# A two-layer transformer block on one core: the weight sums of its seven-product matmuls, and the output sums of its down blocks, made another way

## The chip, the cores and the metric

The kernel runs on one core of a Trainium2 chip. The metric is the device time of one execution in microseconds. Lower is better.

## The reference

Two layers on 512 tokens of width 1024 (batch 1), in float32. Layer 0 mixes tokens by chunked spatial gating, layer 1 by forgetting attention with 12 heads; both add attention on 256 memory rows. Each layer ends in a gated feed-forward of hidden width 2816, which is where the change lies:

```python
f = rmsnorm(h, ln_ffn_pre[layer])
f = (jax.nn.silu(f @ w_ffn_gate[layer]) * (f @ w_ffn_up[layer])) @ w_ffn_down[layer]
h = h + rmsnorm(f, ln_ffn_post[layer])
```

## The kernel before, in words

A float32 product is made of three matmuls in a rounded format: `mm3` multiplies high part by high part, low by high and high by low. `split` makes the parts of a tile: ScalarE rounds it to `hi` (a cast, line 239) and VectorE subtracts, `lo = src - hi` (line 239 too). So each 128x512 block of weights costs one ScalarE and one VectorE instruction before TensorE can use it. The pairs of parts have eight buffers each.

**Sevens.** The feed-forward's gate and up products run as 2x2 block products in seven multiplications instead of eight (the Winograd form of Strassen's scheme). A `Seven` handles two blocks of 128 hidden columns of one weight: it loads two raw tiles of 128x1024 by SyncE's queue (`loaded`, line 144; four raw buffers, so two sevens' worth), which hold the quadrants a11, a12 and a21, a22. `sums` makes four sums of quadrants on VectorE (lines 1040, 1042, 1044, 1045). The products run in the order 1, 7, 6, 2, 5, 4, 3, twelve matmuls each, into three PSUM tiles `x`, `p` and `q`. Between them ScalarE carries a finished partial from one PSUM tile to another (`carry`, line 1055). `end` adds the rest on VectorE (lines 1083 and 1084) and hands the rows on: for a gate, line 1171 and the SiLU of line 1172; for an up, lines 1178 and 1180. `FirstSeven` is the same without the scheme's full chaining, for the first pair of a layer.

**Groups and down blocks.** After the first two hidden blocks, which are done plainly, a layer has five groups of four blocks, made by four sevens: gate, up, gate, up. `Inner` combines each pair of gated rows for the down product (lines 1207 to 1216); for the first pair of a group it makes some low parts "aside", with a transfer on POOL's queue that adds (`split_aside`, `flo`). After each of the first four groups `down_sevens` multiplies by the down weights, again in seven products, each with two units (`DownSeven` a and b, one per pair). Unit a loads its quadrants into two raw tiles, unit b into four plain tiles `wd`. A unit's product `n` on two PSUM outputs is six matmuls 512 wide. The outputs `chain`, `shared`, `lows` and `ups` are two PSUM tiles each. They are added to the eight running sums `ys[tb][dh]` in SBUF in two ways: `put` copies a tile by ScalarE and adds it by transfers on POOL's queue (`y<-yo`, line 1268), and `final` adds it on VectorE (line 1271).

POOL also makes the reciprocal square roots of the norms between the stages (`rsqrt`, line 260), in the same queue as its transfers.

Each engine runs its own instructions strictly in order. The order is made when the program is built: instructions are placed by program order and by when a model of the machine finds their inputs ready, so that an instruction can be placed ahead of an earlier one. `tc.high_priority()` moves instructions forward in this. A wait that lasts longer than modelled holds back whatever is placed behind it on the same engine.

Of the kernel before, what the change touches and what calls it, by code (L numbers as in the profile page):

```python
# [11 lines left out]
ALU = mybir.AluOpType  # L12
# [28 lines left out]
def hybrid(ctx: ExitStack, tc: tile.TileContext, i: dict, out: bass.AP):  # L41
# [20 lines left out]
    def plain(s, shape=(P, T), dt=F32):  # L62
        return yp.tile(list(shape), dt, tag="y", name=name(s))
# [174 lines left out]
    def split(src, hi, lo, eng=None):  # L238
        last_parts[:] = A.copy(hi, src), (eng or V).tensor_sub(lo, src, hi)  # L239
# [22 lines left out]
    class Norm:  # L262
# [31 lines left out]
        def sums(self, tb, cols):  # L294
            return [self.acc[:, c + tb * P : c + (tb + 1) * P] for c in range(0, T, self.width)]
# [722 lines left out]
    class Seven:  # L1018
# [5 lines left out]
        def __init__(self, xs, src, rows):  # L1024
            self.xs, self.rows = xs, rows
            w1, w2 = loaded(src(0)), loaded(src(1))
            self.a = [w[:, d : d + 512] for w in (w1, w2) for d in (0, 512)]
            self.x, self.p, self.q = ps("mm", s="x"), ps("lg", (P, 256), s="a"), ps("tr", (P, 256), s="e")
            self.s1, self.s2 = prob("s1"), prob("s2")

# [5 lines left out]
        def sums(self):  # L1036

            a11, a12, a21, a22 = self.a
            self.s3 = temp("s3")
            V.tensor_add(self.s3, a11, a21)  # L1040
            self.w1 = self.parts(a11)
            V.tensor_add(a21, a21, a22)
            self.w2 = self.parts(a12)
            V.tensor_add(a11, a21, a11)
            V.tensor_add(a12, a11, a12)

        def product(self, o, w, n, more=False):
# [102 lines left out]
    def feed_forward(layer, phase, xp, meanwhile=None):  # L1150
# [36 lines left out]
        def split_aside(src, hi, lo, aside):  # L1187
            if not aside:
                return split(src, hi, lo)
            A.copy(hi, src)  # L1190
            A.activation(lo, hi, AF.Copy, scale=-1.0)
            G.dma_start(lo, src, accum_op=ALU.add)

        class Inner:

            def __init__(self, k, aside):
                self.k, self.aside, self.u = k, aside, {}

            def __call__(self, row, u):
                self.u[row] = u  # L1200
# [19 lines left out]

        class DownSeven:

            def __init__(self, pair, spare):
                self.x = pair.x
                if spare:
                    a11, a12, a21, a22 = (plain("wd").rearrange("p (m c) -> p m c", m=4) for _ in range(4))
                    for n, a in enumerate((a11, a12, a21, a22)):
                        last_load[0] = nc.sync.dma_start(
                            a, i["w_down"][layer, 4 * (n // 2) : 4 * (n // 2) + 4, :, pair.k + n % 2, :].rearrange("m p c -> p m c"))
                else:  # L1230
                    raws = []
                    for dh in range(2):
                        raw = wp.tile([P, 1024], F32, tag="raw", name=name("raw"), bufs=4)
                        last_load[0] = nc.sync.dma_start(
                            raw.rearrange("p (m c) -> p m c", m=4),
                            i["w_down"][layer, 4 * dh : 4 * dh + 4, :, pair.k : pair.k + 2, :].rearrange("m p k c -> p m (k c)"))
                        raws.append(raw.rearrange("p (m k c) -> p m k c", m=4, k=2))
                    a11, a12, a21, a22 = (r[:, :, x, :] for r in raws for x in range(2))
                self.w = {4: a22}
                s3 = temp("s3").rearrange("p (m c) -> p m c", m=4)  # L1240
                V.tensor_sub(s3, a11, a21)
                self.w[1] = self.parts(a11)
                V.tensor_add(a21, a21, a22)
                self.w[2] = self.parts(a12)
                V.tensor_sub(a11, a11, a21)
                V.tensor_add(a12, a11, a12)
                self.w.update({3: a12, 5: a21, 6: a11, 7: s3})

            def parts(self, src):
                pair = pair_of_parts()  # L1250
                split(src, *(t.rearrange("p (m c) -> p m c", m=4) for t in pair))
# [10 lines left out]
        def down_sevens(pairs):  # L1262

            def put(x, *where):
                some = prob("yo")
                A.copy(some, x)  # L1266
                for tb, dh in where:
                    G.dma_start(ys[tb][dh], some, accum_op=ALU.add)  # L1268

            def final(x, tb, dh):  # L1270
                V.tensor_add(ys[tb][dh], x, ys[tb][dh])

            a, b = DownSeven(pairs[0], False), None
            chain = [ps("lg", s="yc") for _ in range(2)]
            a.product(chain, 1, True, False)
            lows = [ps("mm", s="yl") for _ in range(2)]
            a.product(lows, 2, True, False)
            shared = [ps(t, s="ys") for t in ("tr", "tr")]
            a.product(shared, 7, True, False)
            ups = [ps(t, s="yu") for t in ("mm", "lg")]  # L1280
            a.product(ups, 3, True, False)
            b = DownSeven(pairs[1], True)
# [6 lines left out]
            for u in (a, b):  # L1289
                u.product(chain, 6, False, u is b)  # L1290
            for x in range(2):
                A.copy(shared[x], chain[x])
            b.product(ups, 3, False, True)
            for x in range(2):
                final(ups[x], x + 2, 0)
            a.product(chain, 5, False, False)
            a.product(shared, 4, False, False)
            b.product(lows, 2, False, True)
            for x in range(2):
                final(lows[x], x, 0)  # L1300
            b.product(chain, 5, False, True)
            for x in range(2):
                put(chain[x], (x + 2, 0), (x + 2, 1))
            b.product(shared, 4, False, True)
            for x in range(2):
                final(shared[x], x, 1)

        fs = [(act("fhi"), act("flo")) for _ in range(2)]

# [9 lines left out]
        w = [down_weights(layer, 0, dh) for dh in range(2)]  # L1319
# [9 lines left out]
                A.copy(ys[tb][dh], o)  # L1329

        for gi, (k0, k1) in enumerate(groups):
            fs, pairs = [], []
# [25 lines left out]
            down_sevens(pairs)  # L1358


    def layer_b(phase, fp):
# [227 lines left out]
    for tb in range(TB):  # L1589
        end, sums = tail(tb)  # L1590
# [68 lines left out]
```

## Time and profile before

| what | value |
|---|---|
| median of 3 runs | 1103.44 us (1103.33 to 1104.97) |
| the profiled execution's own time | 1101.56 us |
| its span in the trace | 1099.8 us |
| granted TensorE clock, mean | 0.998 |
| TensorE (PE) busy | 1080.4 us, 7266 matmuls |
| VectorE (DVE) busy | 955.7 us |
| ScalarE (ACT) busy | 760.6 us |
| GpSimd (POOL) busy | 107.7 us |
| transfers of the POOL queue (q0, software) | 25.70 MB, 13.3% of the 16 engines' span |
| transfers of the SP queue (q1, hardware) | 116.57 MB, 34.5% |

In rows of the profile a line such as L1040 is a line of the kernel, `out<-in` are its tiles, and the number in brackets at the end of a timeline row is the idle time of the engine before the instruction and what ended it. In rows of windows come the stretch, its length, the busy time of PE, PEld (weight load), DVE, ACT and POOL with counts, the granted clock, the share of the DMA engines and GB/s. In rows of waits come total, times and the longest. Matmuls overlap, so their durations add up to more than the time they take.

### The profile page before, as it was taken

The numbers are of one execution on the slowest core, as the hardware profiler recorded it, in microseconds if no ns is written. First come the engines' busy times: TensorE is split into PE (matmuls) and PEld (weight loads), VectorE is DVE, ScalarE is ACT, GpSimd is POOL, SyncE is SP. The second block draws the span as 40 slices with busy tenths as digits, with TensorE's granted clock in tenths as the row PEclk, the third lists the DMA queues.
The fourth block names the chain that finished last, engine by engine and source line by source line (L and its number), as shares of the span: only waits on it lengthen the run. The fifth ranks groups of instructions, "written<-read, shape, count | busy, mean of one in ns | idle before, by whom it ended". The sixth has DMA issues, their size and how long they took to land.

```text
span 1099.8 us, 19894 instructions
## 1 busy us (share of the span) xinstructions
PE 1080.4 (98%) x7266; PEld 986.5 (90%) x7267; DVE 955.7 (87%) x1906; ACT 760.6 (69%) x1588; POOL 107.7 (10%) x136
## 2 busy tenths in 40 slices
PE   9999999999999989999999999999999999999998
PEld 7998889998989889898988998889998989899896
DVE  7879759999999989896968789868999999989876
ACT  7776578666767657577747788868666766757564
POOL 0000000003030202101000000000003030211200
PEclk9999999999999999999999999999999999999999
DMA  7521331338485655755222654531338575663732
GB/s 270 161 80 52 121 116 39 116 97 211 135 195 150 140 149 133 174 166 162 78 77 65 161 125 122 146 115 39 115 97 200 146 173 139 151 163 93 183 97 77
DMA packets 86298, 143.85 MB, mean 131 GB/s; under 512 B 7028, under 2 KB 50056, under 8 KB 86200
## 3 DMA queue, kind: packets, MB, share of 16 engines
q1 hardware_dynamic: 71480, 116.57, 34.5%
q0 software_dynamic: 14016, 25.70, 13.3%
q8 instruction: 57, 0.93, 0.3%
q10 hardware_dynamic: 704, 0.32, 0.1%
q14 instruction: 41, 0.34, 0.1%
HBM read 105.23 MB, written 2.10 MB: 98 GB/s over the span
## 4 chain that ended last, share of the span: by engine, by line
PE 75%; DVE 9%; DMA 7%; issue 4%; ACT 3%; POOL 1%; SPq 0%; DVEq 0%; ACTq 0%; POOLq 0%
PE y L191 5%; PE y L192 5%; PE y L193 5%; PE ps L191 4%; DMA y<-yo 4%; PE ps L193 4%; PE ps L192 4%; PE a L191 4%; PE a L192 3%; PE a L193 3%; DVE wlo L239 3%; DMA raw<-in_w_gate 3%; PE x L191 2%; PE x L192 2%; PE x L193 2%
## 5 line engine op out<-in xcount | busy, mean ns | idle before, releaser
L239 ACT CAST whi<-raw 128x512 fp32r<-128x512 f32 x444 | 266.2, 619 | 131.3 <-PE x L192 26.2
L239 DVE TENSOR_TENSOR wlo<-raw,whi 128x512 fp32r<-128x512 f32 x444 | 296.4, 686 | 27.2 <-ACT whi L239 25.6
L191 PE MATMUL a<-xshi,whi 128*128 128x256 f32 x320 | 90.6, 283 | 2.5 <-ACT e L1055 2.5
L191 PE MATMUL x<-xshi,whi 128*128 128x256 f32 x320 | 90.6, 283 | 0.0
L192 PE MATMUL x<-xslo,whi 128*128 128x256 f32 x320 | 90.3, 282 | 0.0
L193 PE MATMUL x<-xshi,wlo 128*128 128x256 f32 x320 | 90.2, 282 | 0.0
L193 PE MATMUL a<-xshi,wlo 128*128 128x256 f32 x320 | 89.9, 281 | 0.0
L192 PE MATMUL a<-xslo,whi 128*128 128x256 f32 x320 | 89.8, 281 | 0.0
L1268 POOL DMA_DIRECT2D y<-yo x80 | 69.6, 1265 | 196.3 <-ACT yo L1266 182.4
L191 PE MATMUL ps<-xshi,whi 128*128 128x256 f32 (+1 forms) x224 | 68.4, 305 | 0.0
L192 PE MATMUL ps<-xslo,whi 128*128 128x256 f32 (+1 forms) x224 | 66.6, 298 | 0.0
L193 PE MATMUL ps<-xshi,wlo 128*128 128x256 f32 (+1 forms) x224 | 66.3, 298 | 0.0
L191 PEld LDWEIGHTS a<-xshi,whi 128*128 128x128 f32 x320 | 60.2, 188 | 4.0 <-ACT e L1055 3.6
L191 PEld LDWEIGHTS x<-xshi,whi 128*128 128x128 f32 x320 | 60.8, 190 | 0.2
L192 PEld LDWEIGHTS x<-xslo,whi 128*128 128x128 f32 x320 | 60.8, 190 | 0.0
L193 PEld LDWEIGHTS x<-xshi,wlo 128*128 128x128 f32 x320 | 60.7, 190 | 0.0
L192 PEld LDWEIGHTS a<-xslo,whi 128*128 128x128 f32 x320 | 60.2, 188 | 0.4
L193 PEld LDWEIGHTS a<-xshi,wlo 128*128 128x128 f32 x320 | 60.2, 188 | 0.0
L191 PE MATMUL a<-d2hi,whi 128*128 128x256 f32 x160 | 46.1, 288 | 9.8 <-ACT x L1055 9.8
L191 PE MATMUL y<-whi,mixedhi 128*128 128x512 f32 x128 | 51.3, 401 | 0.0
L192 PE MATMUL y<-wlo,mixedhi 128*128 128x512 f32 x128 | 50.6, 395 | 0.0
L193 PE MATMUL y<-whi,mixedlo 128*128 128x512 f32 x128 | 50.3, 393 | 0.0
(365 smaller groups left out, 3603.4 us busy)
## 6 DMA issues: line engine op xcount, KB each, us to landing
raw<-in_w_gate SPq DMA_DIRECT2D x44, 512.0 KB, 4.1
raw<-in_w_up SPq DMA_DIRECT2D x44, 512.0 KB, 3.6
y<-yo POOLq DMA_DIRECT2D x80, 256.0 KB, 8.2
raw<-in_w_down SPq DMA_DIRECT2D x28, 512.0 KB, 3.9
raw<-in_w_out SPq DMA_DIRECT2D x16, 512.0 KB, 4.0
wd<-in_w_down SPq DMA_DIRECT2D x32, 256.0 KB, 10.8
flo<-s POOLq DMA_DIRECT2D x16, 256.0 KB, 3.4
raw<-in_w_b_q SPq DMA_DIRECT2D x8, 512.0 KB, 4.6
```

Source lines behind the costliest of these rows:

```text
L191: PE.matmul(o, w[0], x[0], start=start, stop=False, skip_group_check=more)
L192: PE.matmul(o, w[0], x[1], start=False, stop=False, skip_group_check=more)
L193: return PE.matmul(o, w[1], x[0], start=False, stop=stop, skip_group_check=more)
L239: last_parts[:] = A.copy(hi, src), (eng or V).tensor_sub(lo, src, hi)
L1268: G.dma_start(ys[tb][dh], some, accum_op=ALU.add)
```

## The change

The sum a21 + a22 of every block is no longer an add on VectorE, but a transfer on POOL's queue, from SBUF to SBUF, that adds a22 onto a21 (`G.dma_start(a21, a22, accum_op=ALU.add)`), issued where the block's loads are. The other sums are rewritten so that each block needs one VectorE sum less (three where there were four in a seven, and three in a down unit). In the down block the products run in another order and in six PSUM tiles instead of eight: `ups` is gone, product 3 is accumulated onto `chain` at the end, and `put` makes eight transfers per group instead of ten. Unit b's loads stand earlier in the program, ahead of the second pair's sevens. ScalarE's copies from PSUM to PSUM stay; those of the down block get high priority.

```diff
 class Seven: __init__
             self.a = [w[:, d : d + 512] for w in (w1, w2) for d in (0, 512)]
+            G.dma_start(self.a[2], self.a[3], accum_op=ALU.add)
 class Seven: sums
             self.s3 = temp("s3")
-            V.tensor_add(self.s3, a11, a21)
             self.w1 = self.parts(a11)
-            V.tensor_add(a21, a21, a22)
+            V.tensor_add(a11, a21, a11)
+            V.tensor_sub(self.s3, a11, a22)
             self.w2 = self.parts(a12)
-            V.tensor_add(a11, a21, a11)
             V.tensor_add(a12, a11, a12)
 class DownSeven
+                G.dma_start(self.a[2], self.a[3], accum_op=ALU.add)
+            def sums(self, pair):
+                self.x = pair.x
+                a11, a12, a21, a22 = self.a
+                self.w = {2: a12, 4: a22}
                 s3 = temp("s3").rearrange("p (m c) -> p m c", m=4)
-                V.tensor_sub(s3, a11, a21)
                 self.w[1] = self.parts(a11)
-                V.tensor_add(a21, a21, a22)
-                self.w[2] = self.parts(a12)
                 V.tensor_sub(a11, a11, a21)
-                V.tensor_add(a12, a11, a12)
-                self.w.update({3: a12, 5: a21, 6: a11, 7: s3})
+                V.tensor_add(s3, a11, a22)
+                self.w.update({5: a21, 6: a11, 7: s3})
 ...
             def product(self, outs, n, start, stop):
                 w = self.w[n]
-                if n > 2:
+                if n == 2:
+                    w = self.parts(w)
+                    V.tensor_add(self.a[1], self.a[0], self.a[1])
+                    self.w[3] = self.a[1]
+                elif n != 1:
                     w = self.parts(w)
 down_sevens, after the change
+            def both(outs, n):
+                a.product(outs, n, False, False)
+                b.product(outs, n, False, True)
+            a, b = us
+            a.sums(pairs[0])
+            chain, shared, lows = ([ps(t, s=n) for _ in range(2)] for t, n in (("tr", "yc"), ("lg", "ys"), ("mm", "yl")))
             a.product(chain, 1, True, False)
+            a.product(shared, 7, True, False)
             a.product(lows, 2, True, False)
+            b.sums(pairs[1])
             b.product(chain, 1, False, True)
             for x in range(2):
                 put(chain[x], (x, 0))
             b.product(shared, 7, False, True)
             for x in range(2):
                 put(shared[x], (x, 1), (x + 2, 1))
+            both(chain, 6)
+            with tc.high_priority():
+                for x in range(2):
+                    A.copy(shared[x], chain[x])
+            b.product(lows, 2, False, True)
+            both(chain, 5)
             for x in range(2):
+                put(chain[x], (x + 2, 1))
             for x in range(2):
+                V.tensor_add(ys[x][0], lows[x], ys[x][0])
+            both(shared, 4)
             for x in range(2):
+                V.tensor_add(ys[x][1], shared[x], ys[x][1])
+            both(chain, 3)
             for x in range(2):
+                V.tensor_add(ys[x + 2][0], chain[x], ys[x + 2][0])
 feed_forward, the loop over a group's pairs
                 if gi < len(groups) - 1:
-                    pairs.append(Inner(m, m < k1 - 2))
+                    pairs.append(Inner(m < k1 - 2))
+                    if m > k0:
+                        downs.append(DownSeven(m, True))
 ...
-            down_sevens(pairs)
+            down_sevens([DownSeven(k0, False)] + downs, pairs)
```

More of the change, by code (lines that the diff above doesn't have):

```diff
@@ L1194, in feed_forward, with __init__ @@
         class Inner:
-            def __init__(self, k, aside):
-                self.k, self.aside, self.u = k, aside, {}
+            def __init__(self, aside):
+                self.aside, self.u = aside, {}
             def __call__(self, row, u):
@@ L1221, in feed_forward, with __init__ @@
         class DownSeven:
-            def __init__(self, pair, spare):
-                self.x = pair.x
+            def __init__(self, k, spare):
                 if spare:
-                    a11, a12, a21, a22 = (plain("wd").rearrange("p (m c) -> p m c", m=4) for _ in range(4))
-                    for n, a in enumerate((a11, a12, a21, a22)):
+                    self.a = [plain("wd").rearrange("p (m c) -> p m c", m=4) for _ in range(4)]
+                    for n, a in enumerate(self.a):
                         last_load[0] = nc.sync.dma_start(
-                            a, i["w_down"][layer, 4 * (n // 2) : 4 * (n // 2) + 4, :, pair.k + n % 2, :].rearrange("m p c -> p m c"))
+                            a, i["w_down"][layer, 4 * (n // 2) : 4 * (n // 2) + 4, :, k + n % 2, :].rearrange("m p c -> p m c"))
                 else:
@@ L1235, in __init__, with parts @@
                             raw.rearrange("p (m c) -> p m c", m=4),
-                            i["w_down"][layer, 4 * dh : 4 * dh + 4, :, pair.k : pair.k + 2, :].rearrange("m p k c -> p m (k c)"))
+                            i["w_down"][layer, 4 * dh : 4 * dh + 4, :, k : k + 2, :].rearrange("m p k c -> p m (k c)"))
                         raws.append(raw.rearrange("p (m k c) -> p m k c", m=4, k=2))
-                    a11, a12, a21, a22 = (r[:, :, x, :] for r in raws for x in range(2))
-                self.w = {4: a22}
+                    self.a = [r[:, :, x, :] for r in raws for x in range(2)]
+                G.dma_start(self.a[2], self.a[3], accum_op=ALU.add)
[3 more added lines that the diff above has]
+                self.w = {2: a12, 4: a22}
                 s3 = temp("s3").rearrange("p (m c) -> p m c", m=4)
-                V.tensor_sub(s3, a11, a21)
                 self.w[1] = self.parts(a11)
-                V.tensor_add(a21, a21, a22)
-                self.w[2] = self.parts(a12)
                 V.tensor_sub(a11, a11, a21)
-                V.tensor_add(a12, a11, a12)
-                self.w.update({3: a12, 5: a21, 6: a11, 7: s3})
-            def parts(self, src):
+                V.tensor_add(s3, a11, a22)
+                self.w.update({5: a21, 6: a11, 7: s3})
+            def parts(self, src, aside=False):
                 pair = pair_of_parts()
-                split(src, *(t.rearrange("p (m c) -> p m c", m=4) for t in pair))
+                split_aside(src, *(t.rearrange("p (m c) -> p m c", m=4) for t in pair), aside)
                 return pair
@@ L1260, in product, with down_sevens @@
                     mm3(o, tuple(t[:, c] for t in self.x[n]), w, start, stop, True)
-        def down_sevens(pairs):
+        def down_sevens(us, pairs):
             def put(x, *where):
@@ L1268, in put @@
                     G.dma_start(ys[tb][dh], some, accum_op=ALU.add)
[L1270 to L1274, printed above, removed]
+            def both(outs, n):
[4 more added lines that the diff above has]
+            chain, shared, lows = ([ps(t, s=n) for _ in range(2)] for t, n in (("tr", "yc"), ("lg", "ys"), ("mm", "yl")))
             a.product(chain, 1, True, False)
-            lows = [ps("mm", s="yl") for _ in range(2)]
+            a.product(shared, 7, True, False)
             a.product(lows, 2, True, False)
[L1278 to L1282, printed above, removed]
+            b.sums(pairs[1])
             b.product(chain, 1, False, True)
@@ L1288, in down_sevens @@
                 put(shared[x], (x, 1), (x + 2, 1))
-            for u in (a, b):
-                u.product(chain, 6, False, u is b)
+            both(chain, 6)
[4 more added lines that the diff above has]
+            both(chain, 5)
             for x in range(2):
-                A.copy(shared[x], chain[x])
-            b.product(ups, 3, False, True)
+                put(chain[x], (x + 2, 1))
             for x in range(2):
[L1295 to L1298, printed above, removed]
+                V.tensor_add(ys[x][0], lows[x], ys[x][0])
+            both(shared, 4)
             for x in range(2):
-                final(lows[x], x, 0)
-            b.product(chain, 5, False, True)
+                V.tensor_add(ys[x][1], shared[x], ys[x][1])
+            both(chain, 3)
             for x in range(2):
[L1303 to L1306, printed above, removed]
+                V.tensor_add(ys[x + 2][0], chain[x], ys[x + 2][0])
         fs = [(act("fhi"), act("flo")) for _ in range(2)]
@@ L1331, in feed_forward @@
         for gi, (k0, k1) in enumerate(groups):
-            fs, pairs = [], []
+            fs, pairs, downs = [], [], []
             for m in range(k0, k1, 2):
```

## The prediction

> **What bounds the kernel now.** I read the page first, for the share of each engine, then the waits of TensorE alone, then a table of windows over one group, then the timeline of each engine around one stall.
>
> ```profile
> span 1099.8 us, 19894 instructions
> PE 1080.4 (98%) x7266; PEld 986.5 (90%) x7267; DVE 955.7 (87%) x1906; ACT 760.6 (69%) x1588; POOL 107.7 (10%) x136
> ```
> ```profile
> PE a L191 <- ACT x L1055: 9.8, 6, 2.1
> PE a L191 <- ACT e L1055: 2.5, 4, 1.0
> ```
> ```profile
> 902.00:962.60 60.60, 59.04 (x419) 55.17 (x419) 57.77 (x104) 41.15 (x80) 10.44 (x13) 1.00 0.63 156
> ```
>
> TensorE is busy 98% of the span, and the diff leaves it as many products. VectorE is second: 87% over the span, but 57.77 of 60.60 us in this group of four sevens and one down block, so inside a group it has some 3 us to spare. What a lighter VectorE can give is therefore only what TensorE now waits for. The first row of waits says 9.8 us and the second 2.5 us, 12.3 us together, all where a product into `p` (a) waits for a carry, ScalarE's copy of one PSUM tile to another. That is the pool. One such stall, seen on all engines, second seven after a down block:
>
> ```profile
> 953.51 10.21 DMA y<-yo
> 965.13 6.52 DMA raw<-in_w_gate
> ```
> ```profile
> 963.82 0.69 DVE L1271 TENSOR_TENSOR y<-ys,y 128x512 f32<-128x512 f32 x1 [0.63 <-DMA y<-yo]
> 971.75 0.69 DVE L1040 TENSOR_TENSOR s<-raw,raw 128x512 f32<-128x512 f32 x1 [2.43 <-DMA raw<-in_w_gate]
> 972.96 0.69 DVE L1042 TENSOR_TENSOR raw<-raw 128x512 f32<-128x512 f32 x1
> 974.16 0.42 DVE L1084 TENSOR_TENSOR s<-a,s 128x256 f32<-128x256 f32 x1
> 975.43 0.69 DVE L1171 TENSOR_TENSOR s<-s,rbc 128x512 f32<-128x512 f32 x1
> 976.15 1.23 ACT L1172 ACTIVATE s<-s 128x512 f32<-128x512 f32 x2 [2.50 <-DVE s L1171]
> 977.28 0.36 ACT L1055 COPY x<-a 128x256 f32<-128x256 f32 x1
> 977.70 0.39 PE L191 MATMUL a<-d2hi,whi 128*128 128x256 f32 x1 [1.78 <-ACT x L1055]
> ```
>
> Read it upwards. TensorE stands 1.78 us for a carry at 977.28; the carry stands behind two SiLUs on ScalarE's queue; these wait 2.50 us for VectorE (L1171, the gate rows of the seven that just ended); VectorE is late because its queue stood 2.43 us at L1040, the weight sum of the seven after next, whose raw tile landed at 971.65. That load took 6.52 us, beside the train of output sums (y<-yo), and was issued late because a VectorE add had stood for one of those sums (963.82). So the chain is: output sums, raw load, VectorE's in-order queue, ScalarE's, TensorE.
>
> **The change part by part.**
>
> ```profile
> DVE s L1040 <- DMA raw<-in_w_gate: 14.6, 8, 2.8
> ```
> ```profile
> 200.03 0.69 DVE L1040 TENSOR_TENSOR s<-raw,raw 128x512 f32<-128x512 f32 x1
> 200.63 0.69 DVE L1045 TENSOR_TENSOR raw<-raw 128x512 f32<-128x512 f32 x1
> ```
> ```profile
> L1040 DVE TENSOR_TENSOR s<-raw,raw 128x512 f32<-128x512 f32 x40 | 27.5, 688 | 14.8 <-DMA raw<-in_w_gate 14.6
> L1268 POOL DMA_DIRECT2D y<-yo x80 | 69.6, 1265 | 196.3 <-ACT yo L1266 182.4 <-DMA y<-yo 10.1 <-DVE y L1271 2.6
> L1192 POOL DMA_DIRECT2D flo<-s x16 | 14.0, 873 | 245.2 <-DVE raw L1045 89.5 <-ACT flo L1191 52.3 <-PE x L192 49.8
> ```
> ```profile
> y<-yo POOLq DMA_DIRECT2D x80, 256.0 KB, 8.2
> flo<-s POOLq DMA_DIRECT2D x16, 256.0 KB, 3.4
> ```
>
> *VectorE's sums.* 40 sevens and 16 down units lose one 128x512 add each, 56 in all. One takes 688 ns, but starts follow each other by 0.60 us, so 34 us of VectorE go. On TensorE's path this is worth nothing by itself: it is cover, 4 sevens and 2 units x 0.60 = 3.6 us more slack in a group that has about 3.
>
> *Output sums.* 80 become 64. POOL issues them in a train and they follow one another: the one in the chain above took 10.21 us to land, where flo, alone, takes 3.4. Two fewer per group stand beside the raw load.
>
> *Weight sums by transfer.* 56 new ones on POOL's queue, so 40 more in net: 40 x 0.873 to 1.265 = 35 to 51 us of an engine that is idle 90% of the time. Each is ready 3.4 us (flo, alone) to 8.2 us (y, in a train) after its raw tile has landed. Before, the sum was an add of 0.6 us. So the second operand of product 7, which is the second of the seven, comes 3 to 8 us later. Is there room?
>
> ```profile
> 965.62 0.69 DVE L1042 TENSOR_TENSOR raw<-raw 128x512 f32<-128x512 f32 x1
> 951.91 0.34 SPq L144 DMA_DIRECT2D raw<-in_w_up  x1
> 974.27 1.59 SPq L144 DMA_DIRECT2D raw<-in_w_up  x2
> 987.87 0.28 PE L191 MATMUL e<-t3hi,whi 128*128 128x256 f32 x1
> 997.85 0.28 PE L191 MATMUL e<-t3hi,whi 128*128 128x256 f32 x1
> ```
>
> Second seven of the group: second tile issued 951.91, its add ran at 965.62; room of 13.7 us, and a load of 6.52 and a sum of 3.4 fit. Third: landed 971.65, sum at 975 to 980, needed by TensorE at 987.87. Fourth: issued by 975.86, landed some 4 to 6.5 us later, sum at 984 to 990, needed at 997.85. So TensorE is never starved of weights by the transfers directly: 0. What they can do is hold VectorE's queue at the add that reads them (a11 = a21 + a11), with the end of the seven before queued behind it (L1084, L1083, L1171, then ScalarE's SiLU and carry). That is the very chain of the stall, so its 12.3 us are the term to size. Bounds: all of it goes if the waiting add is queued behind L1084; it grows if it is queued ahead (rival below: +10.4 us). I take half gone, -6.2 us. For the gain speak that the seven's first VectorE operation no longer needs its second raw tile (product 1 uses a11 alone), so the eight waits of the L1040 row, 14.6 us, end at that place, that the train is shorter, and the 3.6 us of slack. Against it, the 3.4 us that the new sum adds after each landing.
>
> ```profile
> 978.40:981.80 3.40, 3.40 (x19) 3.40 (x18) 3.37 (x6) 1.48 (x4) 0.00 (x0) 0.53 0.12 47
> 981.80:985.00 3.20, 3.20 (x28) 3.20 (x27) 1.61 (x4) 1.51 (x3) 0.00 (x0) 0.96 0.00 0
> ```
>
> *Clock after the stall.* Behind the 1.78 us stall the granted clock was 0.53 for 3.4 us: 19 matmuls where the next window has 28 in 3.2, so they would have taken 2.2 us; 1.2 us were lost, once. Half of it, -0.6; bounds -1.2 and, should another stall be followed so, +1.2. The Trainium skill (TensorE: Matmul & The Clock Gate, Part 1) gives about 3.4 us of idleness as what drops the clock to half; by it a gap of 1.78 us costs nothing and this term is 0, but the rows show the drop, and they decide.
>
> *Order in the down block.* Unit a runs products 1, 7, 2 where it ran 1, 2, 7, 3, so unit b, which needs the group's last gated rows, starts one product earlier.
>
> ```profile
> 943.19 0.39 PE L191 MATMUL yc<-whi,b 128*128 128x512 f32 x1
> 944.58 0.39 PE L191 MATMUL yl<-whi,fhi 128*128 128x512 f32 x1
> 948.41 0.69 DVE L239 TENSOR_TENSOR flo<-s,fhi 128x512 fp32r<-128x512 f32 x1
> 950.94 5.22 POOL L1268 DMA_DIRECT2D y<-yo  x6 [18.71 <-ACT yo L1266]
> 959.40 0.69 DVE L1271 TENSOR_TENSOR y<-yl,y 128x512 f32<-128x512 f32 x1
> ```
>
> A product takes 1.39 us, so b's second (7) would start at 943.19 + 4 x 1.39 = 948.75 where its parts are done at 948.41 + 0.69 = 949.10. It would be 0.35 us late, x8 = 2.8 us; but one sum of 0.6 us ahead of it in VectorE's queue is gone. 0, bounds 0 and +2.8.
>
> *VectorE's last adds.* The add of `lows` ran at 959.40; now it is due after 8 products, at 954.3, while the transfer into the same rows is issued 1.4 us earlier, at 949.5, and lands 5 to 8 us later. VectorE may stand 0.5 to 3.4 us there. The group's 3.6 us of saved adds cover it: 0; without them the next raw loads are issued that much later.
>
> *First pair of a layer, rsqrt, SP's queue.*
>
> ```profile
> 214.27 0.69 DVE L1040 TENSOR_TENSOR s<-raw,raw 128x512 f32<-128x512 f32 x1 [0.83 <-DMA raw<-in_w_gate]
> 223.22 0.28 PE L191 MATMUL e<-t3hi,whi 128*128 128x256 f32 x1
> 174.95 5.07 SPq L144 DMA_DIRECT2D raw<-in_w_up  x2
> 185.71 0.70 POOL L260 TENSOR_TENSOR r<-var,mhalf 128x2 f32<-128x2 f32 x1 [6.98 <-DVE var L291]
> 948.19 2.30 SPq L1228 DMA_DIRECT2D wd<-in_w_down  x2
> ```
>
> The second pair's tile landed at 214.27, its sum would at 217.7, and TensorE wants it at 223.22: 0, at most the 2.2 us that VectorE stands, in two layers +4.4. On POOL a sum waiting for the load issued at 180 (landing 184) stands ahead of the rsqrt at 185.71: free by 1 us; 0. Unit b's loads are written earlier in the program, but SP already issues them as soon as the tiles come free (948.19, within the down block before): 0.
>
> *Sum.* 1101.56 (profiled) - 6.2 - 0.6 = 1094.8. The runs' median, 1103.44, stands 1.9 above the profiled execution, so 1096.6.
>
> **Rivals.**
> *All of the pool goes.* The add that waits is queued behind L1084 everywhere; then -12.3 - 1.2: 1089.9. For it speaks that the waits to end are eight, one a group; against, that carries also wait for SiLUs that no load delays.
>
> *Slower: VectorE stands at the transferred sum.* Place: third seven of each group. If landing is as now, 971.65 + 3.4 = 975.05, where L1042, the add that it replaces, began at 972.96. L1084 comes at 975.05 + 0.6 = 975.65 instead of 974.16; with 0.2 us off for a shorter train, an estimate, the stall grows by 1.3 us: 8 x 1.3 = +10.4, so 1113.8. It decides where the sum lands later than 972.96 with L1084 queued behind it; today's L1084 would have to start by 974.16 - 1.78 = 972.4 for no stall at all. For it speaks that L1040 of that seven stands ahead of L1084 now; against, that program order has L1084 first, so a sum that is expected later may fall behind it. The Trainium skill (DMA: Bandwidth & Descriptors, Issuing engines are not separate DMA queues) says that transfers of SP, ScalarE and POOL interleave on the same 16 engines; by that rule 40 more sums slow the loads, and the trace agrees as far as a load of 6.52 us beside the train goes.
>
> *No change.* VectorE's time is hidden under TensorE, and what the sums give the new landings take back: 1103.4.
>
> **How the numbers follow.** A run can tell about 0.2% (2.2 us) from no change. Half of the pool 0.34 (own range 1093 to 1101), all of it 0.18, no change 0.20, slower 0.28. Faster 0.52, same 0.20, slower 0.28. The range reaches from 1089, the whole pool, to 1112, short of the slower rival's end: about 0.15 is left out.
>
> **What would show it.** Right: the waits of TensorE for L1055 fall from 12.3 to about 6 us; VectorE's busy time falls by some 34 us; its waits for raw loads at the first sum go; POOL has 40 more issues. Wrong: VectorE waiting for a transfer (raw<-raw) by more than the 14.6 us it waited for loads, with SiLU and carry behind it; TensorE waiting in the down block for b's parts; loads of gate and up weights landing later than now.

## The result and the profile after

The changed kernel takes 1171.32 us (median, 1169.8 to 1174.17) where the kernel before takes 1103.38 beside it (1102.41 to 1104.97): 1.0617 times as long, 95% interval 1.0592 to 1.0642. The forecast was 1096.6, faster. The page after:

```profile
span 1168.1 us, 20061 instructions
PE 1101.3 (94%) x7267; PEld 1006.3 (86%) x7267; DVE 932.5 (80%) x1850; ACT 755.7 (65%) x1588; POOL 145.1 (12%) x176
```

TensorE does the same products and is 94% busy instead of 98%. VectorE does have its 56 adds fewer (1906 to 1850 instructions) and POOL its 40 more. The waits of TensorE after (total in us, times, longest):

```profile
PE a L191 <- ACT e L1055: 30.8, 6, 6.6
PE e L191 <- DVE y L1307: 11.2, 6, 3.1
PE x L191 <- ACT x L1055: 10.6, 2, 5.8
PE a L191 <- ACT x L1055: 4.5, 4, 2.5
```

Together 57.1 us, where before two rows gave 12.3. The waits of VectorE, then of ScalarE:

```profile
DVE raw L1042 <- issue: 45.5, 8, 6.4
```
```profile
ACT whi L239 <- DVE s L1043: 77.3, 18, 8.1
```

In the changed file L1042 is `a11 = a21 + a11`, the first add that reads the transferred sum; VectorE stands at it eight times, 45.5 us in all: in seven of the eight groups behind a down block at the second seven (5.0 to 6.4 us), in the last group of layer 1 at the third (4.45 us). In that last group POOL has the second seven's sum ahead of the last two output sums instead of behind them. L1043 makes `s3` from it, and ScalarE, which casts `s3`, stands behind VectorE.

Windows from one down block's start to the next in layer 1, before and after (length, busy time of PE, PEld, DVE, ACT, POOL, granted clock, share of the DMA engines, GB/s):

```profile
821.69:882.18 60.49, 59.95 (x422) 55.50 (x421) 58.95 (x107) 40.09 (x81) 10.36 (x12) 1.00 0.63 157
882.18:943.19 61.01, 59.45 (x423) 55.51 (x421) 58.22 (x105) 41.12 (x80) 10.32 (x12) 1.00 0.62 156
943.19:1006.40 63.21, 61.41 (x423) 57.29 (x422) 57.96 (x103) 41.34 (x80) 10.37 (x12) 0.97 0.61 151
```
```profile
865.48:931.93 66.45, 61.46 (x423) 57.02 (x422) 56.94 (x100) 40.92 (x83) 14.96 (x17) 0.97 0.71 163
931.93:1001.48 69.55, 62.76 (x423) 58.72 (x422) 55.59 (x97) 40.34 (x81) 14.18 (x16) 0.95 0.65 152
1001.48:1070.84 69.36, 61.66 (x422) 57.55 (x421) 55.37 (x97) 40.55 (x81) 14.20 (x16) 0.95 0.65 151
```

These groups are 6.0, 8.5 and 6.2 us longer. Eight of their mean, 6.9, would make 55 of the 68 us, an estimate; the rest lies in the first pairs and in parts that I did not assign. The group that starts at 1001.48, first the queues of SyncE and POOL, then VectorE, ScalarE and TensorE at the stall (the bracket is the idle time before the instruction, and what ended it):

```profile
1010.37 1.50 SPq L144 DMA_DIRECT2D raw<-in_w_up  x2
...
1019.42 0.85 POOL L1273 DMA_DIRECT2D y<-yo  x1 [6.76 <-ACT whi L239]
1024.25 0.84 POOL L1273 DMA_DIRECT2D y<-yo  x1 [3.98 <-DMA y<-yo]
1024.83 1.14 POOL L1028 DMA_DIRECT2D raw<-raw  x1
...
1021.65 0.69 DVE L1304 TENSOR_TENSOR y<-ys,y 128x512 f32<-128x512 f32 x1 [2.23 <-DMA y<-yo]
1023.46 1.28 DVE L1307 TENSOR_TENSOR y<-yc,y 128x512 f32<-128x512 f32 x2
1024.66 1.89 DVE L239 TENSOR_TENSOR wlo<-raw,whi 128x512 fp32r<-128x512 f32 x3
1032.32 0.69 DVE L1042 TENSOR_TENSOR raw<-raw,raw 128x512 f32<-128x512 f32 x1 [5.77 <-issue]
...
1033.82 0.62 ACT L239 CAST whi<-s 128x512 fp32r<-128x512 f32 x1 [7.46 <-DVE s L1043]
1034.35 0.37 ACT L1055 COPY e<-a 128x256 f32<-128x256 f32 x1
...
1034.77 0.58 PE L191 MATMUL a<-xshi,whi 128*128 128x256 f32 x1 [5.97 <-ACT e L1055]
```

Read it upwards, as the stall in the prediction. TensorE stands 5.97 us for a carry of the first seven. The carry has its inputs, but stands on ScalarE behind a cast of the *second* seven's s3, which waits 7.46 us for VectorE. VectorE stands 5.77 us at L1042 for the second seven's transferred sum. That transfer was issued at 1024.83, behind two output sums, the last of which POOL had to hold for 3.98 us until an earlier sum into the same rows was in; VectorE went on at 1032.32, 7.5 us after the issue ("issue" in its bracket means that the profile names no releaser; from issue to landing the trace gives this transfer 7.4 us). The seven's two raw tiles were also loaded later. The first (a11 and a12) was issued at 1010.37, 8.9 us after the down block's start, where before it was 4.1 us after it. The second (a21 and a22), whose halves the transfer adds, was issued at 1011.52, 10.0 us after the start, where before it was 8.7:

```profile
947.29 0.33 SPq L144 DMA_DIRECT2D raw<-in_w_up  x1
948.19 2.30 SPq L1228 DMA_DIRECT2D wd<-in_w_down  x2
951.91 0.34 SPq L144 DMA_DIRECT2D raw<-in_w_up  x1
```

The first tile comes free only when product 3 of unit a has its parts, and product 3 is now the block's last. Two loads for the next unit b are then ahead of it, and both raw tiles are loaded one behind the other. From the down block's start to the sum in place are 30.8 us; before, VectorE's add had it in place after 23.1 us (965.62 and 0.69, less 943.19). The DMA engines were full meanwhile: their share is 1.09 from 1009.48 to 1031.48 and 0.40 in the next 2 us. Before, it was 1.09 too, from 953.19 to 971.19.

Behind the stall, the granted clock:

```profile
1034.80:1037.50 2.70, 2.70 (x13) 2.70 (x14) 1.66 (x3) 0.98 (x2) 0.00 (x0) 0.50 0.28 50
1037.50:1040.70 3.20, 3.20 (x23) 3.20 (x23) 1.85 (x4) 1.51 (x3) 0.00 (x0) 0.77 0.22 45
```

13 matmuls in 2.70 us, where the undisturbed window in the prediction (28 in 3.20) makes 23 or 24; then 23 in 3.20 us. So this stall cost a further 1.2 us and then 0.6, and the mean granted clock of the kernel falls from 0.998 to 0.974.

### The profile page after: what moved, and what is told of

Same layout as the page of the kernel before. It is cut to its first block, busy times and chain, and to the rows that moved or that the text cites. A ratio compares the mean times of both kernels' runs of the same rounds, so it can differ in the third digit from the quotient of the medians.

```text
span 1168.1 us, 20061 instructions
## 1 busy us (share of the span) xinstructions
PE 1101.3 (94%) x7267; PEld 1006.3 (86%) x7267; DVE 932.5 (80%) x1850; ACT 755.7 (65%) x1588; POOL 145.1 (12%) x176
## 4 chain that ended last, share of the span: by engine, by line
PE 45%; DVE 9%; issue 7%; DMA 6%; ACT 2%; POOL 1%; ACTq 0%; DVEq 0%; POOLq 0%
DMA y<-yo 5%; DVE wlo L239 3%; PE a L191 3%; PE a L192 3%; PE a L193 3%; PE y L192 3%; PE y L191 3%; PE y L193 3%; PE e L193 2%; PE e L191 2%; PE ps L191 2%; PE e L192 2%; PE ps L193 2%; PE ps L192 2%; PE x L191 2%
## 5 line engine op out<-in xcount | busy, mean ns | idle before, releaser
L239 DVE TENSOR_TENSOR wlo<-raw,whi 128x512 fp32r<-128x512 f32 x444 | 292.8, 685 | 44.9 <-ACT whi L239 42.6
L239 ACT CAST whi<-raw 128x512 fp32r<-128x512 f32 x444 | 264.3, 618 | 99.5 <-PE a L192 23.4
L191 PE MATMUL a<-xshi,whi 128*128 128x256 f32 x320 | 94.0, 294 | 30.8 <-ACT e L1055 30.8
L191 PE MATMUL x<-xshi,whi 128*128 128x256 f32 x320 | 92.5, 289 | 10.6 <-ACT x L1055 10.6
L192 PE MATMUL a<-xslo,whi 128*128 128x256 f32 x320 | 93.0, 291 | 0.0
L239 ACT CAST whi<-s 128x512 fp32r<-128x512 f32 x56 | 34.6, 618 | 90.0 <-DVE s L1043 77.3
L191 PEld LDWEIGHTS a<-xshi,whi 128*128 128x128 f32 x320 | 63.4, 198 | 32.5 <-ACT e L1055 32.0
L191 PEld LDWEIGHTS x<-xshi,whi 128*128 128x128 f32 x320 | 62.6, 196 | 11.1 <-ACT x L1055 11.0
L1273 POOL DMA_DIRECT2D y<-yo x64 | 55.4, 1176 | 126.3 <-ACT yo L1271 62.5
L1042 DVE TENSOR_TENSOR raw<-raw,raw 128x512 f32<-128x512 f32 x40 | 27.5, 687 | 53.7 <-issue 45.5
L191 PE MATMUL ps<-xshi,whi 128*128 128x256 f32 (+1 forms) x224 | 68.4, 305 | 0.0
L1028 POOL DMA_DIRECT2D raw<-raw x40 | 35.7, 892 | 262.7 <-DVE wlo L239 75.4
L192 PEld LDWEIGHTS a<-xslo,whi 128*128 128x128 f32 x320 | 63.5, 198 | 0.4
L193 PEld LDWEIGHTS a<-xshi,wlo 128*128 128x128 f32 x320 | 63.7, 199 | 0.0
L191 PE MATMUL e<-t3hi,whi 128*128 128x256 f32 x160 | 46.0, 287 | 11.2 <-DVE y L1307 11.2
```

The source lines that it names most:

```text
L191: PE.matmul(o, w[0], x[0], start=start, stop=False, skip_group_check=more)
L192: PE.matmul(o, w[0], x[1], start=False, stop=False, skip_group_check=more)
L193: return PE.matmul(o, w[1], x[0], start=False, stop=stop, skip_group_check=more)
L1028: G.dma_start(self.a[2], self.a[3], accum_op=ALU.add)
```

## The experiments

Each number stands against the kernel before on the same chip: ratio and 95% interval. Line numbers shift by a few between these kernels.

**1. All weight sums on VectorE, the new down block kept.**

```diff
-            G.dma_start(self.a[2], self.a[3], accum_op=ALU.add)      # Seven and DownSeven
+            V.tensor_add(a21, a21, a22)                              # in sums of both
```

> All weight sums a21 + a22 go back to VectorE (four adds per seven and per down unit), the new down block with its eight output sums stays. Theory Q (queue: the second seven's weight sum stands on POOL's queue behind the last output sums, and VectorE and ScalarE stand behind it in order): only the waits of product 7 for the drained chain tile stay, 11.2 us of the 57.1 us that TensorE waits in the changed kernel; 1100 to 1117 us. Theory D (the down block's new order and its PSUM tiles are what costs): 1150 us or more. Theory B (48 more transfers slow all the transfers): 1100 to 1117 us too.

1117.32 us, 1.0129 [1.0112, 1.0146]: at the upper end of theories Q and B, far below D's.

**2. The transfers of the sevens kept, the old down block.** The down block's part of the diff is taken back, its 16 transfers with it.

```diff
-            down_sevens([DownSeven(k0, False)] + downs, pairs)
+            down_sevens(pairs)                                       # and DownSeven, down_sevens as before
```

> The sevens keep their weight sums as transfers; the down block is the old one (ten output sums, VectorE's sums, the old order of products). Theory Q: four output sums of the last put stand ahead of the second seven's weight sum instead of two, so it is slow still, 1150 to 1190 us. Theory D: 1098 to 1108 us. Theory B: 1150 us or more, no matter where in the group the transfers stand.

1145.47 us, 1.0383 [1.0347, 1.0418], outside all three ranges, nearest to Q's and B's. So the sevens' transfers cost 3.8% without the new down block, and the new down block, with the rewritten order of a seven's sums that run 1 keeps, 1.3% without transfers; together they cost 6.2%, a little more than the sum. Both halves of the change lose as they are placed here. In run 2 the waits of TensorE were again those for a carry:

```profile
PE a L191 <- ACT e L1055: 27.9, 10, 4.9
PE x L191 <- ACT x L1055: 9.9, 2, 6.8
```

In run 1 they were others, and only in some groups. Its waits, then windows of three groups of layer 1:

```profile
PE e L191 <- DVE y L1307: 15.0, 4, 4.7
```
```profile
834.34:895.85 61.51, 60.46 (x422) 55.37 (x421) 58.30 (x104) 39.35 (x80) 8.60 (x10) 1.00 0.58 146
895.85:957.72 61.87, 60.07 (x423) 55.73 (x422) 57.84 (x104) 39.26 (x80) 8.59 (x10) 1.00 0.57 145
957.72:1024.64 66.92, 62.18 (x423) 57.82 (x422) 58.15 (x104) 40.55 (x82) 8.60 (x10) 0.95 0.53 134
```

The same program text gives groups of 61.5 and of 66.9 us. VectorE's rows in the second and in the third of them:

```profile
912.42 0.68 DVE L1304 TENSOR_TENSOR y<-ys,y 128x512 f32<-128x512 f32 x1
...
917.79 0.68 DVE L1307 TENSOR_TENSOR y<-yc,y 128x512 f32<-128x512 f32 x1
...
922.00 0.68 DVE L1041 TENSOR_TENSOR raw<-raw 128x512 f32<-128x512 f32 x1
...
979.40 0.69 DVE L1041 TENSOR_TENSOR raw<-raw 128x512 f32<-128x512 f32 x1 [5.45 <-DMA raw<-in_w_up]
980.61 1.28 DVE L1304 TENSOR_TENSOR y<-ys,y 128x512 f32<-128x512 f32 x2
983.01 1.28 DVE L1307 TENSOR_TENSOR y<-yc,y 128x512 f32<-128x512 f32 x2
```

In the good group the second seven's first sum (L1041) is placed behind the adds that empty the down block's PSUM tiles (L1304, L1307). In the bad one it is placed ahead of them, and VectorE stands 5.45 us at it for a raw load (issued from 967.57 on), with both adds, on which TensorE depends, behind it.

**3. Only the second seven of each group on VectorE**, the seven at which VectorE stood.

```diff
+                V.tensor_add(a21, a21, a22)          # first up seven of a group; no transfer there
```

> Only the second seven of each group (the first up product behind a down block, 8 of the 40) makes its weight sum on VectorE again; the other 32 and the 16 of the down units stay transfers. Theory Q: the stalls of 4 to 7 us at that seven go (30.8 + 10.6 + 4.5 us of TensorE's waits and the clock dips behind them), the 11.2 us of product 7 stay: 1108 to 1125 us. Theory D: 1160 us or more. Theory B: a sixth of the transfers less, so a sixth of the 68 us: about 1160 us.

1150.06 us, 1.0422 [1.0397, 1.0448], far slower than I had expected and outside all three ranges. VectorE's waits and TensorE's:

```profile
DVE raw L1044 <- DMA raw<-in_w_up: 40.7, 8, 6.6
```
```profile
PE e L191 <- DVE y L1310: 27.2, 6, 6.1
```

The 45.5 us at the transferred sum became 40.7 at the raw load, and now the adds of the chain stood behind. The load itself lands later than VectorE's place for the sum; which engine makes the sum decides only who stands for it, and where.

**4. The sum one place ahead on POOL**, between the last two output sums.

```diff
+            with tc.high_priority():
+                G.dma_start(self.a[2], self.a[3], accum_op=ALU.add)
```

> Every seven's weight sum stays a transfer, but is given high priority, which moves it one place ahead on POOL's queue behind a down block: between the last two output sums instead of behind both. Theory Q: it is issued some 4 us earlier (the second output sum stood 3.98 us for an earlier landing), the stall of about 6 us falls to 2 to 3 us in the groups: 1130 to 1150 us. Theories D and B: no change, 1165 to 1177 us.

1146.92 us, 1.0404 [1.0383, 1.0424], as theory Q said. The place behind the held output sum was worth some 24 us of the 68.

**5. Unit a's parts of product 3 made early**, so that its raw tile comes free.

```diff
+                self.early = not spare
...
-                    self.w[3] = self.a[1]
-                elif n != 1:
+                    self.w[3] = self.parts(self.a[1]) if self.early else self.a[1]
+                elif n != 1 and not (n == 3 and self.early):
```

> The changed kernel with unit a's parts of product 3 made right behind those of product 2, so that its first raw tile comes free some two products' worth earlier, as in the kernel before. The next group's first up seven (second seven behind the down block) gets its loads issued about 4 us after the down block's start again, not 8.9. Theory L (the late load of that seven is what VectorE and the transferred sum stand for): its weight sum is queued and landed some 5 us earlier, the 6 us waits of TensorE for its carry go, 45.5 us of VectorE at the add that reads the transferred sum fall under 15, and the time falls from 1171 to 1125 to 1140. Theory Q (the sum stands in POOL's queue behind the output sums, whenever its tile has landed): the sum still comes behind the train, waits of VectorE there stay near 40 us, 1160 to 1171.

1133.14 us, 1.0265 [1.0213, 1.0318]: 38 us back, inside theory L's range. But the run moved two things, not one. In the group that begins at 968.08 the first raw tile of the second seven is again issued early, 3.7 us after the down block's start; the second, which the transfer reads, 9.9 us after it, about as late as in the change (10.0). And in five of the eight groups the second seven's sum now stands on POOL ahead of the last two output sums (here at 987.26, ahead of 987.80 and 989.65), where the change has it behind them; there the gain is of the load and of the place together. The first group of each layer keeps the change's order on POOL, and there the earlier load shows without a new place: VectorE's stand at the second seven falls from 6.4 to 1.7 us in layer 0 and from 5.3 to 2.4 us in layer 1, where the group falls from 66.45 to 62.30 us.

VectorE still stood 24.6 us in all, where L said under 15. The chain of waits in the group that begins at 968.08 shows where (start, us, what):

```profile
991.89 7.87 DMA raw<-in_w_gate
...
1000.32 1.29 DMA raw<-raw
1001.62 4.73 issue
1006.34 0.70 DVE raw L1042
...
1008.99 0.28 ACT e L1055
1009.31 0.39 PE a L191
```

Now, in all groups but the first of each layer, it is the *third* seven, a gate: its load takes 7.87 us, beside the last output sum (issued at 989.65, 7.5 us to landing) and unit b's weight sum. Its own sum takes 6.0 (1000.32 to 1006.3); by then the output sums have landed, and what runs beside it is the two loads of the fourth seven (issued from 998.41 on, landed about 1006). The same queue follows: L1042, carry, TensorE.

**6. All sums on VectorE, `shared` and `chain` exchanged in PSUM.**

```diff
-(("tr", "yc"), ("lg", "ys"), ("mm", "yl"))
+(("lg", "yc"), ("tr", "ys"), ("mm", "yl"))
```

> All weight sums on VectorE, the new down block kept, and its PSUM tiles exchanged: shared in tr and chain in lg, so that the two tiles that product 7 of the next seven needs are drained one product earlier and the chain of product 3 holds tiles of which there are three. Theory R (the 15 us for which TensorE waits for the last adds of the chain, line 1307, come of the tiles' choice): that wait falls under 4 us, 1117 to 1102 to 1106. Theory L (VectorE stands at the late raw load with those adds behind it, so any add that drains a tile is late): the wait moves to the other add or to the carry, 1112 to 1118.

1114.23 us, 1.0085 [1.0058, 1.0111], against 1.0129 of run 1: the wait for the chain's adds is gone from the list, and groups that were 66.9 us are 65.7. The wait turned into one for weight parts (`PE e L191 <- ACT whi L239`, longest 2.4 us), behind the same stand of VectorE at the late load, 21.1 us in all. The time is in theory L's range; the tiles' choice is worth about a third of run 1's loss.

**7. All sums on VectorE, product 3's parts early.** The diffs of 1 and 5 together.

> All weight sums on VectorE, the new down block kept with its tiles as in the change, and unit a's parts of product 3 made right behind those of product 2 (raw tile free early). Theory L: VectorE's 5.45 us at the first sum of the first up seven fall under 2 us, the adds behind it run on time, TensorE's 15 us for line 1307 go: 1117 to 1102 to 1106. Theory R: the last adds are still the last work of the block and drain the two tiles that the second product of the next seven needs, wait of 2 us or more in each group: 1110 to 1117.

1122.68 us, 1.0161 [1.0123, 1.0200]: missed, no better than run 1. The early tile moved the choice of the planner, the program that places the instructions: now two groups of layer 1 had the sum ahead of the adds, with 67.2 and 68.2 us, and one did not, with 59.6.

**8. Early parts, sum ahead and exchanged tiles, transfers kept.** The diffs of 4, 5 and 6 together.

> The change with its transfers kept and three repairs together: weight sum one place ahead on POOL (alone it gave 1147), product 3's parts early (raw tile free early), shared in tr and chain in lg. If places in the queues and the late load are the whole loss (theories Q, L, R together), TensorE's waits for carries and adds fall from 57 to under 15 us and the time is 1100 to 1112. Theory B (40 more transfers of 256 KB on the 16 engines make every load and every sum late, whatever their order): waits stay over 30 us, 1130 to 1147.

1138.37 us, 1.0301 [1.0258, 1.0343]; no better than run 5, and in theory B's range, with 30.5 us of TensorE's waits for carries. Once the load is early, neither more priority on POOL, where run 5 already has the sum ahead in most groups, nor the tiles' choice is worth anything that shows: the stand at the transferred sum is left (`DVE raw L1043 <- issue`, 22.6 us), mostly at the third seven. In runs 3 and 7 VectorE stood at a raw load with ready adds behind it, in run 8 at a transferred sum with the cast and the carry behind; that the planner reckoned with an earlier landing is my reading, its model was not looked into. So the order was fixed by hand.

**9. All sums on VectorE; the second seven's first sum placed behind the chain's last adds.** `drained` holds those adds and is emptied after that seven.

```diff
-            V.tensor_add(a21, a21, a22)
+            with behind(held):                       # held = drained in the first up seven of a group
+                V.tensor_add(a21, a21, a22)
...
-                V.tensor_add(ys[x + 2][0], chain[x], ys[x + 2][0])
+                drained.append(V.tensor_add(ys[x + 2][0], chain[x], ys[x + 2][0]))
```

> All weight sums on VectorE, the new down block as in the change, and one order fixed: the first sum of a group's first up seven is placed on VectorE behind the last adds of the down block (line of the chain), which empty the PSUM tiles that the next seven writes. Without that order (1117) the first two down blocks of a layer were followed by the next after 60.5 to 61.9 us and the third after 68.8 and 66.9 us; in the third and fourth the planner had put that sum ahead of the adds, and TensorE waited 15 us for them. Theory V (VectorE's order, one late operand ahead of adds that are ready): all groups take 60.5 to 62 us, no wait for the last adds, 1098 to 1105. Theory L (the late load starves the second seven in any order): the wait turns into one for that seven's parts, 1108 to 1118.

**10. The same with product 3's parts early** (diff of 5).

> The same fixed order with unit a's parts of product 3 made early as well, so that the up seven's raw tile comes free earlier. Theory V: both together leave TensorE nothing to wait for in a group; the sums on VectorE and the new down block then cost what the kernel before costs less its 12.3 us of waits, 1092 to 1101. Theory L: no better than the fixed order alone, or worse by the split that stands ahead of others on VectorE, 1103 to 1115.

Run 9: 1099.99 us, 0.9963 [0.9946, 0.9980]. Run 10: 1096.14 us, 0.9928 [0.9912, 0.9944], faster than both kernels of this case. Both are in theory V's ranges. Run 9 against run 1 is one order on one engine, some 17 us. The windows of layer 1 in run 9, then the engines of run 10 and the largest of TensorE's waits in it:

```profile
822.38:883.90 61.52, 60.47 (x422) 55.40 (x421) 58.31 (x104) 39.35 (x80) 8.61 (x10) 1.00 0.58 146
883.90:944.69 60.79, 60.10 (x422) 55.71 (x421) 57.86 (x104) 39.28 (x80) 8.60 (x10) 1.00 0.58 148
944.69:1005.63 60.94, 60.83 (x422) 55.72 (x421) 57.85 (x104) 40.21 (x81) 8.61 (x10) 1.00 0.58 147
```
```profile
PE 1082.4 (99%) x7267; PEld 984.0 (90%) x7267; DVE 956.7 (87%) x1906; ACT 752.1 (69%) x1588; POOL 93.4 (9%) x120
```
```profile
PE ys L191 <- ACT whi L239: 2.4, 2, 1.2
```

The groups are even, the clock is 1.00 in these of run 9, and TensorE's waits for carries are down to one of 0.2 us in run 10, with VectorE as busy as before (956.7 against 955.7 us) and no transferred weight sum at all. The new down block costs nothing once VectorE's order suits it. VectorE's stand at raw loads is nearly gone as well: 21.8 us at the up loads in run 1, 4.9 at all gate and up loads in run 9, which did nothing for the load. So the load was late only for the place that the sum had.

**11. Early parts (diff of 5), transfers kept except in the third seven.**

```diff
+            if moved:                                # not in the second gate seven of a group
+                G.dma_start(self.a[2], self.a[3], accum_op=ALU.add)
...
+            if not self.moved:
+                V.tensor_add(a21, a21, a22)
```

> The change with product 3's parts early (1133 alone), and of its transfers those of each group's third seven (second gate) made on VectorE again; the other three sevens and the down units keep theirs. With product 3 early VectorE stood 1.8 to 4.7 us in every group at the third seven's transferred sum, whose load (9 us) and sum (6 us) follow each other beside the output sums. Theory Q and L (only a sum that lands beside the output sums costs anything): 1105 to 1115. Theory B (the other 46 transfers slow the loads too): VectorE stands at that seven's raw load instead, 1118 to 1133.

1119.07 us, 1.0135 [1.0113, 1.0156]: in theory B's range, and with the sign that B named, in VectorE's row:

```profile
DVE raw L1044 <- DMA raw<-in_w_gate: 17.4, 8, 4.4
```

The stand moved from the sum to the raw load, as in run 3; it is 17.4 us where the kernel before had 14.6 at the same load. The planner was free to place that sum again, so this run doesn't tell traffic from order; the next one fixes the order.

**12. Run 10 with 36 of the 56 transfers**: first and fourth seven and down units by transfer, second and third on VectorE, the third's sum placed behind the first seven's end.

```diff
+            if moved:                                # first and fourth seven
+                G.dma_start(self.a[2], self.a[3], accum_op=ALU.add)
...
-                held[:] = () if opens else drained
+                held[:] = drained or ends[:1]        # ends[0]: the end of the seven before last
```

> The fixed order and the early parts of product 3 (1096 with all sums on VectorE), and 36 of the 56 weight sums by transfer again: those of the first and fourth seven of each group and of the down units. The second and the third seven of a group, whose loads run beside the output sums, keep their sum on VectorE; the third's is placed behind the first seven's end. Theory S (a transferred sum costs only where VectorE stands at it with other work behind, and VectorE's time is hidden otherwise): 1092 to 1099, waits of TensorE as without transfers. Theory B (36 more transfers of 256 KB slow the loads of the others): VectorE stands at the raw loads of the second or third seven again by more than 10 us in all, 1101 to 1112.

1097.89 us, 0.9953 [0.9937, 0.9969]: theory S. VectorE has 18.1 us less to do than in run 10 and waits only 1.4 us in all for raw loads, and the kernel isn't faster for it.

```profile
PE 1080.3 (99%) x7267; PEld 985.1 (90%) x7267; DVE 938.6 (86%) x1870; ACT 754.6 (69%) x1588; POOL 127.3 (12%) x156
```

So 36 more transfers, with the third seven's sum held in its place, change the time by 0.25% against run 10, and the intervals of the two overlap. The Trainium skill (DMA: Bandwidth & Descriptors, Issuing engines are not separate DMA queues) has all transfers interleave on the same engines. The rows of the loads agree with that for the gate weights: with transfers and early parts they land after 4.6 to 5.3 us in the median (runs 5, 8, 11 and 12), without transfers after 4.0 (runs 7 and 10). They don't for the up weights: 5.3 us in the change, but 5.6 in run 1 without any weight transfer, and 3.5 in run 2 with 40 of them and the old down block; so the transfers are not what delays these. The rival's "40 more sums slow the loads" thus holds for the gate loads, by 0.6 to 1.3 us, and run 12 shows that it need not cost time. That the other 20 transfers cost what they do by their place, in the stretch in which the DMA engines are full, and by VectorE's order around them is inferred: no run puts these 20 alone back.

## Why the prediction was wrong

*The step that failed* is the one under "Weight sums by transfer": "room of 13.7 us, and a load of 6.52 and a sum of 3.4 fit", 0 for the second seven. These 9.9 us, from the issue of the second raw tile to the sum in place, measured 20.8 (1011.52 to 1032.32). The prediction compared the sum with the time of the add that it replaces, in the order of before, and took the three times from three places of the old trace. In the new kernel both raw tiles were loaded one behind the other among full DMA engines, the output sums stood ahead of the sum on POOL until 1024.83, and the sum took 7.5 us instead of 3.4. So VectorE stood 5.0 to 6.4 us there in seven of the eight groups. The groups are 6.0 to 8.5 us longer, in which the waits for L1307 and the slower clock are contained too.

*SP's queue* was costed at 0 with the argument that loads are issued when tiles come free. That was the right rule and I did not ask when they come free: product 3's move to the end holds unit a's first raw tile. Run 5, which frees it, gains 38 us, part of which comes of the place on POOL that changed with it; the size of the load alone stays open.

*Stalls*, -6.2: the chain was named rightly (VectorE in order, ScalarE in order, carry), its sign was not. The rows for L1055 went from 12.3 to 45.9 us. That they can go is shown by runs 9 and 10, but by placing the sums, not by moving them.

*The slower rival* had the mechanism, with the wrong place and price: third seven and +1.3 us a group, where the kernel had the second seven in seven of eight groups and a stand of 5.0 to 6.4 us. The third seven did come, as the next in line, when run 5 took the second away. I weighed "program order has L1084 first" against it; the traces show work whose operand is late standing ahead of work that is ready, on VectorE in run 1 (L1041 ahead of L1304 and L1307) and on ScalarE here (the cast ahead of the carry).

*VectorE's sums*: "worth nothing by itself" was right, and run 12 shows it. The 3.6 us a group that they were to give as cover for *VectorE's last adds* did not cover them: at the adds of `lows` (L1301), which the prediction meant, VectorE stood 0.6 to 1.5 us in six waits, inside the forecast 0.5 to 3.4, but also up to 2.9 us at those of `shared` (L1304, 13.1 us in all), which it did not have. L1307, behind them on VectorE, empties the two `tr` tiles that product 7 of the next seven writes. The prediction had an add and not the tile; TensorE's row for L1307 is 11.2 us, longest 3.1.

*Clock*, -0.6: the drop behind a stall did come, and the sign was wrong, with more and longer stalls instead of fewer. That it follows a short stall is not shown as a rule: in the same trace of before it followed the one of 1.78 us and not those of 1.56 and 2.07 us. *POOL* had 40 more issues and 37.4 us more busy time, inside 35 to 51. *Order in the down block*, 0 to +2.8: 0, as no row of TensorE's waits in the changed kernel names a product into `yc`, `ys` or `yl`. *First pair*, at most +4.4 in two layers: the value taken, 0, was wrong and the bound nearly reached. VectorE stood there twice (`DVE raw L1042 <- DMA raw<-raw`, 7.9 us, 2 times), and TensorE behind it 2.47 and 1.62 us.

That run 10 takes what was forecast is chance in the number: it has the new down block without the transfers on which the forecast rested. What stays open: whether run 10's 7.7 us come from the new down block or only from the order that the held sum gives; the kernel before with its own third seven's sum held was not run. More raw buffers, which would take the late load away at its root, were not tried. How much of the 7.5 us of the sum, in the stretch in which the DMA engines are full, is contention was not measured by itself.

## What to carry to other kernels

When an operation off the critical path is handed to a transfer, add up its operand's whole way in the new kernel (when the buffer comes free, what is ahead in both queues, landing among other transfers), and compare it with the place of its reader in an in-order queue, not with the time at which TensorE needs the result. When the same code gives groups of two lengths, compare the order of one engine's instructions in a good and a bad group: one late operand ahead of ready work cost 5 to 8 us a group in run 1, and one explicit order gave it back in run 9. Time taken from an engine that is hidden is worth nothing, even where, as in run 12, the transfers that replace it cost nothing that shows.

## What the runs showed of the hardware

A 256 KB transfer that adds within SBUF, 3.3 us in the median from issue to landing in the changed kernel, took 7.5 us behind two others of its kind, with the DMA engines' share at 1.09. A gap of 5.97 us in TensorE's work was followed by a granted clock of 0.50 for 2.7 us, like the gap of 1.78 us before (0.53 for 3.4 us); gaps of 1.56 and 2.07 us before were followed by 1.00 (916.10 to 919.50, 1041.40 to 1045.00). In run 9 no group's window that was taken shows less than 1.00. The Trainium skill (TensorE: Matmul & The Clock Gate, Part 1) has the clock fall after a window of about 3.4 us without work: the gap of 5.97 us agrees with that, as do those of 1.56 and 2.07 us; the one of 1.78 us does not.
